# Rotary embedding on one core: the cast of the first f32 rows ahead of the position fetches on ScalarE, and a wait among GpSimd's loads

## The chip, the cores and the metric

One core of a Trainium2 chip. The metric is the device time of one execution in microseconds. Profiled times below count from the start of the span, which is 1.8 us shorter than the device time (83.6 against 85.36 us for the profiled run of before).

## The reference

```python
def reference(x, freqs, positions):          # x: 8 x 8 x 1024 x 64 f32
    half = x.shape[-1] // 2
    angles = np.outer(positions, freqs)      # 1024 x 32
    cos, sin = np.cos(angles), np.sin(angles)
    x_first, x_second = x[..., :half], x[..., half:]
    return np.concatenate([x_first * cos - x_second * sin,
                           x_first * sin + x_second * cos], axis=-1)
```

16.8 MB are read and 16.8 MB written. The sines and cosines are the same for all 64 heads, so they are computed once.

## The kernel before

The data is cut in eight tiles of 128 partitions x 64 rows x 64 values. GpSimd's loads turn f32 into bf16 on the way and its stores turn bf16 back into f32. The first 16 rows of tile 0 come by two f32 loads from SyncE and are cast by ScalarE; the last 24 rows of tile 7 (the "tail") are computed in f32 and stored by SyncE.

```python
    x0 = singles.tile([P, head, d], f32)                 # head = 16 rows, piece = 8
    for r in range(0, head, piece):
        nc.sync.dma_start(out=x0[:, r:r + piece], in_=hbm(x, 0, r, r + piece))
    # ... pos_i, fr cleared ...
    nc.scalar.dma_start(out=pos_i[...], in_=positions)   # cut
    nc.scalar.dma_start(out=fr[0:P:32], in_=freqs[None, :].to_broadcast([P // 32, half]))
    for g in range(ntiles):                              # 8 loads, one queue
        lo = 0 if g else head
        nc.gpsimd.dma_start(out=xts[g][:, lo:], in_=hbm(x, g, lo))
    # ... VectorE: shuffle pos_i and fr, turns = pos * freq / 2pi, minus its whole part ...
    nc.scalar.activation(out=sin_h, in_=turns, func=Sin, scale=twopi)
    nc.scalar.activation(out=whole, in_=turns, func=Abs)
    nc.scalar.activation(out=cos_h, in_=whole, func=Sin, scale=-twopi, bias=half_pi)
    nc.scalar.copy(out=xts[0][:, :head], in_=x0)
    # ... rotate(): four products, a difference and a sum on VectorE, per tile ...
    tail = 3 * piece
    for g in [1, 0] + list(range(2, ntiles)):
        # ... rotate, then
        nc.gpsimd.dma_start(out=hbm(out, g, 0, hi), in_=ot)
    # ... SyncE waits for the GpSimd stores but the last, then stores the tail in pieces of 8 rows
```

## Time and profile before

| | before |
|---|---|
| device time, median | 85.37 us (85.36 to 85.39, 3 runs) |
| f32 rows landed, both halves | 11.46 us |
| first product on VectorE | 17.13 us |
| loads done, last completion | 43.2 us |
| VectorE done | 73.7 us |
| DMA packets done | 82.3 us |

The prediction below shows the lines that carry the argument. The page's row of what the DMA moved in each of 40 slices (GB/s, one slice 2.09 us):

```profile
GB/s 0 182 202 259 227 208 227 204 227 208 212 220 208 227 208 227 204 212 223 200 388 423 423 455 400 470 388 463 408 439 439 416 455 423 455 392 422 431 331 70
```

Loads count on their bf16 side, so some 215 is full speed there and some 430 for stores; the step at the 21st value is where loads end and stores begin.

A line of the waits (us, times, longest): VectorE waited only 1.9 us for the frequencies, once.

```profile
DVE fr L77 <- DMA fr<-in_freqs_dram: 1.9, 1, 1.9
```

### The profile page before, as it was taken

How to read it: one execution, taken by the hardware profiler on the slowest of the kernel's cores; microseconds unless marked ns; L12 is line 12 of the kernel's file. 1: busy time of each engine (PE TensorE's matmuls, PEld its weight loads, DVE VectorE, ACT ScalarE, POOL GpSimd, SP SyncE). 2: the span in 40 equal slices, each digit the busy share in tenths (PEclk: the TensorE clock that was granted, in tenths of full speed). 3: DMA queues.
4: the chain of work that ended last, by engine and by line, in shares of the span. 5: the costliest groups of instructions: out<-in, count | busy, mean ns of one | idle time of the engine just before them, and what ended most of it. 6: DMA issues, size and time to landing. Idle time of an engine off the chain costs nothing.

```text
span 83.6 us, 163 instructions
## 1 busy us (share of the span) xinstructions
DVE 63.5 (76%) x66; ACT 9.3 (11%) x6; POOL 8.7 (10%) x20
## 2 busy tenths in 40 slices
DVE  1024995089999999999999999999999999920000
ACT  0000049999000000000000000000000000000000
POOL 4960000000002001002002002000100202000000
DMA  0899999999999999999999999999999999999992
GB/s 0 182 202 259 227 208 227 204 227 208 212 220 208 227 208 227 204 212 223 200 388 423 423 455 400 470 388 463 408 439 439 416 455 423 455 392 422 431 331 70
DMA packets 3065, 25.45 MB, mean 304 GB/s; under 512 B 360, under 2 KB 376, under 8 KB 1144
## 3 DMA queue, kind: packets, MB, share of 16 engines
q0 software_dynamic: 2304, 24.12, 94.2%
q1 hardware_dynamic: 720, 1.31, 5.1%
q10 hardware_dynamic: 40, 0.01, 0.0%
q14 instruction: 1, 0.01, 0.0%
HBM read 16.79 MB, written 16.78 MB: 402 GB/s over the span
## 4 chain that ended last, share of the span: by engine, by line
DVE 67%; DMA 12%; ACT 7%; DVEq 1%; SPq 1%; issue 0%; ACTq 0%
DMA x<-in_x_dram 12%; DVE t L114 11%; DVE t L115 11%; DVE ot L119 10%; DVE ot L117 10%; DVE ot L116 10%; DVE ot L118 10%; ACT sin_h L96 2%; ACT L96 2%; ACT L101 2%; ACT xt L101 1%; DVEq L170 1%; DVE last L117 1%; DVE last L118 1%; DVE last L116 1%; SPq L56 1%
## 5 line engine op out<-in xcount | busy, mean ns | idle before, releaser
L114 DVE TENSOR_TENSOR t<-xt,sin_h 128x2048 bf16<-128x2048 bf16 (+2 forms) x9 | 9.9, 1099 | 3.5 <-ACT sin_h L96 3.5
L128 POOL DMA_DIRECT2D out_dram<-ot x8 | 4.2, 526 | 60.4 <-DVE ot L119 60.4
L115 DVE TENSOR_TENSOR t<-xt,sin_h 128x2048 bf16<-128x2048 bf16 (+2 forms) x9 | 9.9, 1099 | 0.0
L117 DVE TENSOR_TENSOR ot<-xt,cos_h 128x2048 bf16<-128x2048 bf16 (+1 forms) x8 | 9.3, 1167 | 0.0
L119 DVE TENSOR_TENSOR ot<-ot,t 128x2048 bf16<-128x2048 bf16 (+1 forms) x8 | 9.3, 1167 | 0.0
L116 DVE TENSOR_TENSOR ot<-xt,cos_h 128x2048 bf16<-128x2048 bf16 (+1 forms) x8 | 9.3, 1166 | 0.0
L118 DVE TENSOR_TENSOR ot<-ot,t 128x2048 bf16<-128x2048 bf16 (+1 forms) x8 | 9.3, 1166 | 0.0
L74 POOL DMA_DIRECT2D xt<-in_x_dram x8 | 4.3, 577 | 0.8 <-PEq L170 0.8
L76 DVE LOAD_MASK_SELECT pos_i<-pos_i x1 | 0.0, 14 | 3.8 <-DMA pos_i<-in_positions_dram 3.8
L101 ACT ACT_TABLE_LOAD x1 | 1.3, 1283 | 11.5 <-DMA x<-in_x_dram 11.5
L87 DVE TENSOR_TENSOR turns<-pos_f,fturn 128x2048 f32<-128x2048 f32 x1 | 2.3, 2293 | 0.0
L93 DVE TENSOR_TENSOR turns<-turns,whole 128x2048 f32<-128x2048 f32 x1 | 2.3, 2293 | 0.0
L99 ACT ACTIVATE cos_h<-whole,half_pi 128x2048 bf16<-128x2048 f32 x1 | 2.0, 2003 | 0.0
L96 ACT ACTIVATE sin_h<-turns 128x2048 bf16<-128x2048 f32 x1 | 1.9, 1909 | 0.0
L98 ACT ACTIVATE whole<-turns 128x2048 f32<-128x2048 f32 x1 | 1.9, 1893 | 0.0
L77 DVE LOAD_MASK_SELECT fr<-fr x1 | 0.0, 14 | 1.9 <-DMA fr<-in_freqs_dram 1.9
L96 ACT ACT_TABLE_LOAD x1 | 1.3, 1283 | 0.0
L91 DVE TENSOR_SCALAR whole<-turns 128x2048 f32<-128x2048 f32 x1 | 1.2, 1226 | 0.0
L101 ACT CAST xt<-x 128x1024 bf16<-128x1024 f32 x1 | 1.0, 1045 | 0.0
L117 DVE TENSOR_TENSOR last<-xt,cos_h 128x768 f32<-128x768 bf16 x1 | 0.9, 950 | 0.0
L119 DVE TENSOR_TENSOR last<-last,t 128x768 f32<-128x768 f32 x1 | 0.9, 950 | 0.0
L116 DVE TENSOR_TENSOR last<-xt,cos_h 128x768 f32<-128x768 bf16 x1 | 0.9, 949 | 0.0
(12 smaller groups left out, 2.6 us busy)
## 6 DMA issues: line engine op xcount, KB each, us to landing
out_dram<-ot POOLq DMA_DIRECT2D x7, 2048.0 KB, 18.5
xt<-in_x_dram POOLq DMA_DIRECT2D x7, 1024.0 KB, 25.2
out_dram<-ot POOLq DMA_DIRECT2D x1, 1280.0 KB, 11.2
xt<-in_x_dram POOLq DMA_DIRECT2D x1, 768.0 KB, 7.6
out_dram<-last SPq DMA_DIRECT2D x3, 256.0 KB, 3.6
x<-in_x_dram SPq DMA_DIRECT2D x2, 256.0 KB, 6.9
pos_i<-in_positions_dram ACTq DMA_DIRECT2D x1, 8.0 KB, 3.7
fr<-in_freqs_dram ACTq DMA_DIRECT2D x1, 0.5 KB
```

The costliest lines, as they stand in the source:

```text
L74: nc.gpsimd.dma_start(out=xts[g][:, lo:], in_=hbm(x, g, lo))
L87: nc.vector.tensor_mul(out=turns, in0=pos_f.to_broadcast([P, C, half]), in1=fturn.to_broadcast([P, C, half]))
L93: nc.vector.tensor_sub(out=turns, in0=turns, in1=whole)
L96: nc.scalar.activation(out=sin_h, in_=turns, func=Sin, scale=twopi)
L101: nc.scalar.copy(out=xts[0][:, :head], in_=x0)
L114: v.tensor_mul(out=t1, in0=xf, in1=sin)
L115: v.tensor_mul(out=t2, in0=xs, in1=sin)
L116: v.tensor_mul(out=of, in0=xf, in1=cos)
L117: v.tensor_mul(out=os_, in0=xs, in1=cos)
L118: v.tensor_sub(out=of, in0=of, in1=t2)
L119: v.tensor_add(out=os_, in0=os_, in1=t1)
L128: nc.gpsimd.dma_start(out=hbm(out, g, 0, hi), in_=ot)
```

## The change

In short, ScalarE first casts the f32 rows and only then fetches positions and frequencies, and GpSimd queues two loads, waits for those rows, and queues the other six. The diff has a third part: the tail shrinks from 24 rows to 16.

```diff
--- before.py
+++ after.py
@@ -56,22 +56,27 @@
         nc.sync.dma_start(out=x0[:, r:r + piece], in_=hbm(x, 0, r, r + piece))
 
 
+    for g in range(ntiles):
+        lo = 0 if g else head
+        if g == 2:
+            tc.keep_in_program_order(nc.gpsimd.keepalive_nop(ins=[nc.gpsimd.lower_ap(x0)]))
+        tc.keep_in_program_order(nc.gpsimd.dma_start(out=xts[g][:, lo:], in_=hbm(x, g, lo)))
+
+
+
+    tc.keep_in_program_order(nc.scalar.copy(out=xts[0][:, :head], in_=x0))
     i32 = mybir.dt.int32
     words = mybir.dt.size(positions.dtype) // 4
     pos_i = singles.tile([P, C, words], i32)
     nc.vector.memset(pos_i, 0)
-    nc.scalar.dma_start(
+    tc.keep_in_program_order(nc.scalar.dma_start(
         out=pos_i[0:P:group].bitcast(positions.dtype),
         in_=bass.AP(tensor=positions.tensor, offset=positions.offset,
-                    ap=[[C, chunks], [1, C], [1, 1]]))
+                    ap=[[C, chunks], [1, C], [1, 1]])))
     fr = singles.tile([P, half], f32)
     nc.vector.memset(fr, 0.0)
-    nc.scalar.dma_start(out=fr[0:P:32], in_=freqs[None, :].to_broadcast([P // 32, half]))
-
-
-    for g in range(ntiles):
-        lo = 0 if g else head
-        nc.gpsimd.dma_start(out=xts[g][:, lo:], in_=hbm(x, g, lo))
+    tc.keep_in_program_order(
+        nc.scalar.dma_start(out=fr[0:P:32], in_=freqs[None, :].to_broadcast([P // 32, half])))
 
     nc.vector.stream_shuffle(pos_i, pos_i, [i // group * group for i in range(32)])
     nc.vector.stream_shuffle(fr, fr, [0] * 32)
@@ -98,8 +103,6 @@
     nc.scalar.activation(out=whole, in_=turns, func=mybir.ActivationFunctionType.Abs)
     nc.scalar.activation(out=cos_h, in_=whole, func=Sin, scale=-twopi, bias=half_pi)
 
-    nc.scalar.copy(out=xts[0][:, :head], in_=x0)
-
     v = nc.vector
 
     def rotate(g, lo, hi, ot):
@@ -118,7 +121,7 @@
         v.tensor_sub(out=of, in0=of, in1=t2)
         v.tensor_add(out=os_, in0=os_, in1=t1)
 
-    tail = 3 * piece
+    tail = 2 * piece
     ots = []
     for g in [1, 0] + list(range(2, ntiles)):
         hi = C if g < ntiles - 1 else C - tail
```

## The prediction

> **What bounds the kernel now.** I read the page's second part first, because the time before (85.37 us, with a span of 83.6 us) leaves the question whether VectorE, busy 76%, or the DMA is the bound. The rows of 40 slices (2.09 us each) answer it:
>
> ```profile
> DVE  1024995089999999999999999999999999920000
> ACT  0000049999000000000000000000000000000000
> DMA  0899999999999999999999999999999999999992
> ```
>
> The DMA is full from the second slice to the last but one; VectorE stands still in the last four slices and has holes in the first eight. The windows view (columns: busy us of each engine, clock, DMA share, GB/s) splits the DMA time:
>
> ```profile
> 2.00:42.00 40.00, 31.61 (x31) 9.32 (x6) 5.14 (x10) 1.00 1.02 215
> 42.00:82.00 40.00, 31.73 (x33) 0.00 (x0) 2.61 (x5) 1.00 1.05 421
> ```
>
> The first 40 us move the input (215 GB/s is counted on the bf16 side of the casting loads, so about 430 of f32), the second 40 us the output. Loads and big stores share one GpSimd queue, so they run in issue order. The packet records in the trace agree: loads to 42.9 us, the first store's packets from 42.4 us, and each full tile 4.86 us, load or store. So the bound is one chain of 80 us of transfers, and the printed chain that ended last (67% VectorE) is only the other long path. How far apart the two are is in the timeline:
>
> ```profile
> 17.13 1.22 DVE L114 TENSOR_TENSOR t<-xt,sin_h 128x2048 bf16<-128x2048 bf16 x1 [3.46 <-ACT sin_h L96]
> ...
> 26.59 0.54 POOL L128 DMA_DIRECT2D out_dram<-ot  x1 [21.05 <-DVE ot L119]
> ...
> 65.20 0.52 POOL L128 DMA_DIRECT2D out_dram<-ot  x1 [6.29 <-DVE ot L119]
> ...
> 69.61 0.52 POOL L128 DMA_DIRECT2D out_dram<-ot  x1 [3.89 <-DVE ot L119]
> ...
> 72.78 0.95 DVE L119 TENSOR_TENSOR last<-last,t 128x768 f32<-128x768 f32 x1
> 77.84 2.27 SPq L141 DMA_DIRECT2D out_dram<-last  x3
> ```
>
> The first store is queued at 26.59 us but moves at 42.4. This lead shrinks, because VectorE makes a tile every 6.81 us and the DMA stores one in 4.86. The seventh store, queued at 65.20, moves at 71.64; the eighth, queued at 69.61, at 76.50 (both from the packet records). VectorE could thus start late by a few microseconds at no cost. This slack decides the case.
>
> **What the Trainium skill says.**
> 1. "DMA: Bandwidth & Descriptors", Queues, rings and completion order: each DMA engine takes turns between its rows, a packet at a time. The trace agrees: the second half of the f32 rows, issued at 1.47 us, lands only at 11.46 us (the chain has "DMA x<-in_x_dram" for 9.99 us), since each of its 2 KB packets (0.09 us) takes turns with a load packet of 0.47 to 0.6 us.
> 2. "Perfetto Trace Analysis", Per-engine timelines: a ScalarE instruction is pushed into a wait queue and the sequencer goes on; a sequencer-only instruction waits on the sequencer itself. A DMA after the cast therefore need not wait for the cast to end, but does wait for a semaphore wait that stands as its own instruction. The trace has this for the f32 rows (a step "ACTq L101" of 0.02 us at 11.48, ahead of the table load). Whether a DMA passes a running activation, no line of the before trace shows.
> 3. "ScalarE: Activation LUTs", What ACT_TABLE_LOAD costs: 1283 ns, plus about 1380 ns of drain. The trace has 1283 ns twice, and no drain: the cast starts 1.30 us after its load, the sine 1.29 us after its own.
> 4. "DMA: Bandwidth & Descriptors", Where 436 GB/s comes from: a ceiling of 435 GB/s. The trace's 430 and 421 are near it, so no reordering can make the 80 us much shorter.
>
> **The change part by part.** The lines that carry it:
>
> ```profile
> 1.03 0.60 ACTq L63 DMA_DIRECT2D pos_i<-in_positions_dram  x1
> 1.27 4.27 POOL L74 DMA_DIRECT2D xt<-in_x_dram  x8 [0.83 <-PEq L170]
> 1.67 1.14 ACTq L69 DMA_DIRECT2D fr<-in_freqs_dram  x1
> 7.35 0.01 DVE L77 LOAD_MASK_SELECT fr<-fr  x1 [1.91 <-DMA fr<-in_freqs_dram]
> 11.37 2.29 DVE L93 TENSOR_TENSOR turns<-turns,whole 128x2048 f32<-128x2048 f32 x1
> 11.53 1.28 ACT L101 ACT_TABLE_LOAD   x1 [11.53 <-DMA x<-in_x_dram]
> 12.83 1.04 ACT L101 CAST xt<-x 128x1024 bf16<-128x1024 f32 x1
> 13.89 1.28 ACT L96 ACT_TABLE_LOAD   x1
> ```
>
> 1. *When the f32 rows land (X).* Before, the second half's packets began only at 5.2 us, between those of positions (3.48) and frequencies (6.16), though it was issued at 1.47. The order suggests that SyncE's and ScalarE's requests are served in turn. Without ScalarE's two, the second half should follow the first, which ends at 4.0 us: eight packets per engine, each beside a load packet, 8 x (0.47 + 0.10) = 4.6 us, to 8.6; the before run took 0.95 us from last data to landing, hence X = 9.4 us (11.5 if this reading is wrong).
>
> 2. *GpSimd's wait.* It resumes at X. Load 3 is wanted when load 2 ends, 13.1 to 13.7 us. The first load needed 2.2 us from issue to packets (1.27 to 3.50), so load 3 is ready at 11.7. Free. At X = 11.5 it would be 13.8, a hole of at most 0.6 us.
>
> 3. *Positions and frequencies.* ScalarE passes its wait at X, pushes table load and cast, and issues positions at X + 0.15, frequencies 0.65 us later. From issue to packets the idle path took 1.45 us (f32 rows: 0.75 to 2.20) and, on the full DMA, 1.6 us (last stores: 77.84 to 79.44). Then data waits for a load packet (0.3 to 0.6), the completion for another (0.6), and 0.35 us more to land: X + 3.8. Sharing a ring with positions can add up to 1 us; I take X + 4.3, so frequencies land at F = 13.7 us instead of 7.3.
>
> 4. *The angle chain.* From 7.35 to 13.66 VectorE took 6.31 us for its angle work; then the sine's 1.91 us and 0.1 of hand-overs. The sine's table load, which held the sine until 15.18 before, is over by X + 3.8 = 13.2 and leaves the path. First product at F + 8.35 = 22.05 us, late by D = 22.05 - 17.13 = 4.9 us.
>
> 5. *Tail of 16 rows instead of 24.* Start spacings give 0.069 us + 0.521 ns per bf16 element (2048: 1.136; 768: 0.469) and twice the slope for f32 output (768: 0.869). The last tile takes 6x0.736 + 2x0.469 + 4x0.869 = 8.83 us before and 6x0.869 + 2x0.336 + 4x0.602 = 8.29 after: 0.54 saved on VectorE. The eighth store grows to 48 rows and is queued 6x0.133 = 0.8 us later, at 70.41 + D. One of three last stores falls away.
>
> 6. *The end.* With 2.0 to 2.2 us from queue to packets (as the first load), store 7 can move at 67.3 + D, against 71.64: free while D is under 4.3. Store 8 can move at 72.5 + D, against 76.50: free while D is under 4.0. VectorE ends at 73.73 - 0.54 + D = 78.1, and its two last stores run beside store 8. After store 8 starts there remain 8 packets of 12 KB per engine at about 0.485 us and 16 of 2 KB at 0.086: 5.3 us, against 5.84 before (76.50 to 82.34), of which some 0.3 us are really saved. With D = 4.9: 77.4 + 5.3 + 0.2 of skew = 82.9, against 82.34: +0.6 us.
>
> Sum: nothing removed from the 80 us of transfers, about -0.3 for the smaller tail, +0.9 for the part of the delay beyond its slack. 85.37 + 0.6 = **86.0 us**.
>
> **The rivals.**
> - *ScalarE's DMA waits for the cast to finish.* The table load and cast take 1.28 + 1.05 + 0.02 us, so all moves 2.35 us: D = 7.2, time 88.2 us (+3.3%). For it: one instruction stream, and the change's own words "casts, then fetches". Against it: item 2 of the skill, with cast's inputs ready at that point.
> - *The f32 rows land no earlier (X = 11.5).* D = 7.0 and perhaps a hole in the loads: 87.9 to 88.3 us. For it: taking turns with load packets explains most of its 10 us. Against: the silent gap from 4.0 to 5.2 us. Both rivals together give some 90 us, where VectorE plainly sets the end.
> - *The fetches pass the wait.* If the separate wait is for the first half of the rows (landing at 4.55) and the cast carries the other, positions go out at 4.7, F is 9, D about 0.3, and only the tail counts: 85.0 us. Against it: before, the cast's separate wait ended at 11.46, with the second half.
> - *A gain at the start* (f32 rows unhindered, DMA full earlier): the DMA row is already 8 in its second slice, so at most about 1 us can be gained there.
>
> **Range and chances.** My reading has about half the weight, and lies between 85.2 and 86.8 with the uncertainty of F; a limit of 2% is 87.08 us. The two slower rivals have about a third, nearly all of it beyond 2%. The fetches passing the wait has a tenth. A gain of 2% would be 1.7 us of 85.4, with the transfers untouched: hardly possible. Range 85.0 to 88.3; chances 0.02 faster, 0.60 within 2%, 0.38 slower.
>
> **What would show it.** In the after timeline: table load of the cast near 9.4 us (step 1); third GpSimd load queued there and no dip in the DMA row near 13 us (2); positions issued beside the table load, not after the cast (3); frequencies' shuffle near 13.7 (3); first product near 22 us (4); last tile's pieces 128x1536 and 128x512 (5); DMA row still full or with one thin slice near 77 us, VectorE ending near 78 (6). A cast at 12.8 as before, or positions issued after the cast, makes it slower; DMA dips through the last 20 us would show VectorE as the bound.

## More of the kernel before

Next, the windows view of two stretches that turn out to matter (stretch, length, busy VectorE, ScalarE and GpSimd, clock, DMA share, GB/s):

```profile
12.00:16.00 4.00, 1.66 (x1) 3.96 (x4) 0.00 (x0) 1.00 1.04 217
40.00:46.00 6.00, 6.00 (x6) 0.00 (x0) 0.52 (x1) 1.00 1.04 343
```

In the first, two loads are done and the third begins; the second holds the turn from loads to stores.

## The result, and the profile after

The changed kernel took 88.93 us (median of 4 runs, 88.63 to 89.09), the kernel before in the same rounds 85.38 us. The ratio is 1.040, with a 95% interval of 1.036 to 1.044. It is slower by 3.6 us, outside the predicted range of 85.0 to 88.3.

The same rows of the page of the changed kernel (a slice is now 2.18 us):

```profile
DVE  0000000299919999999999999999999999999500
ACT  0000087000099500000000000000000000000000
DMA  0999999999999999999999999999999996698992
GB/s 0 217 203 244 233 205 172 200 218 203 218 207 230 203 222 222 207 215 211 154 403 414 444 437 429 437 407 452 407 456 429 399 399 264 279 452 331 435 367 72
```

Two things are new in the DMA row: thin slices at 6, 6 and 8 near its end, where VectorE is now busy almost to the end. That is a DMA that waits for VectorE. And there is a smaller dent of 172 GB/s in the seventh slice. The windows (columns as above) put numbers on it:

```profile
12.00:16.00 4.00, 0.51 (x3) 2.73 (x3) 2.70 (x6) 1.00 0.98 178
40.00:46.00 6.00, 6.00 (x6) 0.00 (x0) 0.25 (x1) 1.00 1.02 262
42.00:86.00 44.00, 39.77 (x40) 0.00 (x0) 3.14 (x6) 1.00 0.99 386
```

The output half of the run takes 44 us at 386 GB/s instead of 40 at 421. The timeline (start, length, engine, line, what, and in brackets the idle time before it and what ended it) shows what VectorE waited for:

```profile
11.12 1.28 ACT L67 ACT_TABLE_LOAD   x1 [11.12 <-DMA x<-in_x_dram]
11.19 0.60 ACTq L72 DMA_DIRECT2D pos_i<-in_positions_dram  x1
11.60 3.10 POOL L63 DMA_DIRECT2D xt<-in_x_dram  x6 [9.16 <-DMA x<-in_x_dram]
11.83 1.10 ACTq L79 DMA_DIRECT2D fr<-in_freqs_dram  x1
12.41 1.04 ACT L67 CAST xt<-x 128x1024 bf16<-128x1024 f32 x1
...
17.41 0.01 DVE L82 LOAD_MASK_SELECT fr<-fr  x1 [1.47 <-DMA fr<-in_freqs_dram]
...
25.70 1.23 DVE L117 TENSOR_TENSOR t<-xt,sin_h 128x2048 bf16<-128x2048 bf16 x1 [1.98 <-ACT sin_h L101]
...
73.78 0.52 POOL L131 DMA_DIRECT2D out_dram<-ot  x1 [6.29 <-DVE ot L122]
...
78.99 0.52 POOL L131 DMA_DIRECT2D out_dram<-ot  x1 [4.69 <-DVE ot L122]
...
81.80 1.24 SPq L144 DMA_DIRECT2D out_dram<-last  x2
```

Everything that hangs on the f32 rows starts at 11.1 us, not at 9.4 as predicted. The fetches are issued beside the table load and ahead of the cast, so they do not wait for it. The frequencies are there 5.6 us after their issue. The first product is 8.57 us late (25.70 against 17.13), and so is the store of every whole tile: the seventh is queued at 73.78 us, and by the packet records it moves at 74.87. A full store takes 4.86 us and the sixth began at 68.08, so the DMA engines that were ahead could have begun the seventh at 72.9 (the last packet of the sixth ended at 74.66): they wait for VectorE.

### The profile page after: what moved, and what is told of

It is laid out like the page before. It is cut to its first block, busy times and chain, and to the rows that moved or that the text cites. A ratio compares the mean times of both kernels' runs of the same rounds, so it can differ in the third digit from the quotient of the medians.

```text
span 87.0 us, 162 instructions
## 1 busy us (share of the span) xinstructions
DVE 63.0 (72%) x66; ACT 9.3 (11%) x6; POOL 8.7 (10%) x20
## 4 chain that ended last, share of the span: by engine, by line
DVE 71%; DMA 17%; ACT 3%; SPq 1%; DVEq 1%; issue 0%; ACTq 0%
DMA x<-in_x_dram 11%; DVE t L117 11%; DVE t L118 11%; DVE ot L120 10%; DVE ot L122 10%; DVE ot L119 10%; DVE ot L121 10%; DMA fr<-in_freqs_dram 6%; DVE turns L98 3%; DVE turns L92 3%; ACT sin_h L101 2%; DVE whole L96 1%; ACT L67 1%; SPq L56 1%; DVEq L173 1%; DVE last L120 1%
## 5 line engine op out<-in xcount | busy, mean ns | idle before, releaser
L67 ACT ACT_TABLE_LOAD x1 | 1.3, 1283 | 11.1 <-DMA x<-in_x_dram 11.1
L101 ACT ACT_TABLE_LOAD x1 | 1.3, 1283 | 0.0
L120 DVE TENSOR_TENSOR last<-xt,cos_h 128x512 f32<-128x512 bf16 x1 | 0.7, 689 | 0.0
L122 DVE TENSOR_TENSOR last<-last,t 128x512 f32<-128x512 f32 x1 | 0.7, 689 | 0.0
```

The costliest lines, as they stand in the source:

```text
L67: tc.keep_in_program_order(nc.scalar.copy(out=xts[0][:, :head], in_=x0))
L120: v.tensor_mul(out=os_, in0=xs, in1=cos)
L122: v.tensor_add(out=os_, in0=os_, in1=t1)
```

## The experiments

Twelve kernels ran, all correct; six of them are the remaining combinations of the change's three parts. Kernels ran together with new runs of the kernel before, whose medians were 85.28 to 85.41 us. "First product" is the start of VectorE's first product in the profiled run, "loads done" the last completion of the eighth load in the trace.

| kernel | tail | fetches | GpSimd's wait | first product | loads done | time, median |
|---|---|---|---|---|---|---|
| before | 24 | first | none | 17.13 | 43.24 | 85.38 |
| tail alone | 16 | first | none | 17.12 | 43.24 | 85.39 |
| wait alone | 24 | first | third load | 17.11 | 45.86 | 87.73 |
| wait and tail | 16 | first | third load | 16.59 | 46.48 | 88.01 |
| late fetches alone | 24 | after rows | none | 26.06 | 43.43 | 89.99 |
| late fetches and tail | 16 | after rows | none | 26.04 | 43.54 | 89.17 |
| late fetches and wait | 24 | after rows | third load | 26.04 | 45.89 | 89.63 |
| changed | 16 | after rows | third load | 25.70 | 45.88 | 88.93 |

### Fetches first again (wait and tail kept)

```diff
-    tc.keep_in_program_order(nc.scalar.copy(out=xts[0][:, :head], in_=x0))
     ... the two fetches on ScalarE ...
+    tc.keep_in_program_order(nc.scalar.copy(out=xts[0][:, :head], in_=x0))
```

> The changed kernel with the cast moved behind the two fetches on ScalarE, so positions and frequencies are fetched at once again; GpSimd's wait and the tail of 16 rows stay. Theory (the late fetches alone cost the 3.6 us, by starting the products 8.6 us late): frequencies land near 7.3 us, first product near 17 us, time 85.0 to 85.6 us. Rival (GpSimd's wait, which leaves a hole in the loads near 13 us and lets one DMA engine trail, costs a part): 86 to 88 us although the first product is at 17 us.

Measured: 88.01 us (87.63 to 88.30, 4 runs), ratio to before 1.031 (1.028 to 1.034). The first product is back at 16.59 us and VectorE ends at 72.7, yet the time falls by only 0.9 us. That is at the upper edge of the rival's range. My theory, that the late fetches alone cost the 3.6 us, fell here in its simple form: with them undone, something else holds the end.

### The wait alone

```diff
     for g in range(ntiles):
         lo = 0 if g else head
+        if g == 2:
+            tc.keep_in_program_order(nc.gpsimd.keepalive_nop(ins=[nc.gpsimd.lower_ap(x0)]))
-        nc.gpsimd.dma_start(...)
+        tc.keep_in_program_order(nc.gpsimd.dma_start(...))
```

> The kernel before with GpSimd's wait ahead of the third load alone. Theory: hole of 0.2 to 0.7 us in the loads, which the full DMA cannot give back: 85.4 to 86.1 us. Rival (the wait costs a good part of the 3.6 us): 86.5 us or more. VectorE's first product stays at 17.1 us either way.

Measured: 87.73 us (87.11 to 88.42), ratio 1.028 (1.022 to 1.033). The rival held. Its windows:

```profile
12.00:16.00 4.00, 1.83 (x1) 3.96 (x4) 3.10 (x6) 1.00 1.00 188
40.00:46.00 6.00, 6.00 (x6) 0.00 (x0) 0.52 (x1) 1.00 0.98 238
```

From 12 to 16 us the DMA moves 188 GB/s instead of 217: 0.5 us of work lost on average (4 us x 29/217). But a load is done only when the last of its 16 parts is. The Trainium skill ("DMA: Bandwidth & Descriptors", Why a DMA increments its semaphore by 16 and not by 1) says that each of the 16 DMA engines posts its own completion, and the trace has 16 completion records for every load. Before, those of the third load lie between 18.30 and 18.84 us; with the wait, between 18.67 and 19.86, so the last is 1.0 us late. The gap stays through the seventh load (39.33 against 38.30): nothing evens the engines out here. At the turn from loads to stores another 1.6 us are lost (last completion of the eighth load 45.86 against 43.24, 238 GB/s instead of 343), with single packets of up to 1.6 us where 0.63 is usual. This second loss is not only the latest part's: the earliest part of the eighth load is 1.6 us late too (44.42 against 42.82). The stores then follow at the old pace, and the whole end is 2.4 us later.

### The wait one load later

```diff
-        if g == 2:
+        if g == 3:
```

> The kernel before with GpSimd's wait for the f32 rows ahead of the fourth load, so three loads are queued instead of two. Theory (the wait costs because two loads run out at 13 us, just as the third is being queued, and a DMA engine that falls behind there stays behind): the queue never runs dry, the loads end near 42.9 us as before, time 85.2 to 85.7 us. Rival (the stop and restart of GpSimd's issuing costs by itself, or waiting on the rows does): about 87 to 88 us as with the wait ahead of the third load.

This is the kernel with the wait alone, but with three loads queued ahead of it. Measured: 85.33 us, ratio 1.000 (0.998 to 1.002). Its windows are close to those of before:

```profile
12.00:16.00 4.00, 1.49 (x1) 3.96 (x4) 1.88 (x4) 1.00 1.08 225
40.00:46.00 6.00, 6.00 (x7) 0.00 (x0) 0.52 (x1) 1.00 1.06 337
```

So neither the wait nor the restart of GpSimd's issuing costs; letting the queue run dry does. Two loads last until 12.8 to 13.7 us, and the third was issued at 12.0 us with the wait alone, with its first packet at 13.2 (11.6 and 12.8 in the changed kernel).

### The late fetches alone

```diff
-        if g == 2:
-            tc.keep_in_program_order(nc.gpsimd.keepalive_nop(...))       # in the changed kernel
-    tail = 2 * piece
+    tail = 3 * piece
```

> The changed kernel without GpSimd's wait and with the tail of 24 rows of before, so only the order on ScalarE is changed. Theory: first product 8 to 9 us late as in the changed kernel, and VectorE's end, now 0.5 us later for the larger tail, sets the time: 89.0 to 89.7 us. Rival (the wait carries a part): 86 to 88 us.

Measured: 89.99 us (89.86 to 90.07), ratio 1.054 (1.052 to 1.056). Without any wait, and with the loads done at 43.43 us as before, it is slower than the changed kernel, and slightly more than expected. Two lines of its timeline matter for the fetches:

```profile
11.06 0.60 ACTq L70 DMA_DIRECT2D pos_i<-in_positions_dram  x1
16.77 0.01 DVE L79 LOAD_MASK_SELECT pos_i<-pos_i  x1 [15.72 <-DMA pos_i<-in_positions_dram]
```

The positions are the first request on ScalarE's queue, and yet they take 5.7 us. Their first packet moves at 14.92 us, 3.86 us after the issue. In the changed kernel, where GpSimd's third load is issued only after them (11.60 against 11.19 us), it is 1.59 us.

### The changed kernel with the old tail

```diff
-    tail = 2 * piece
+    tail = 3 * piece
```

> The changed kernel with the tail of 24 rows of before. If VectorE sets the end of the changed kernel, its 0.54 us more of work show fully or are partly given back by the smaller eighth store: 89.0 to 89.6 us. If the DMA still sets the end, it is the 0.3 us of a third small store: 89.2 us at most, with no later VectorE end visible in the time. The same as the changed kernel (88.9) would say that the tail is worth nothing in this state.

Measured: 89.63 us (89.59 to 89.85), ratio 1.051. The smaller tail goes with 0.7 us by the medians and 1.06 by the profiled runs (89.85 - 88.79), of which 0.34 is a later first product in this run (26.04 against 25.70). What is left, 0.4 to 0.7 us, is about VectorE's 0.5: VectorE sets the end here.

### The changed kernel without its wait

```diff
-        if g == 2:
-            tc.keep_in_program_order(nc.gpsimd.keepalive_nop(ins=[nc.gpsimd.lower_ap(x0)]))
```

> The changed kernel with GpSimd's wait taken out and nothing else, which completes the table of four at a tail of 16 rows: neither part 85.39, wait alone 88.01, both 88.93. If the later of two ends counts (the wait's cost lies under the late fetches'), taking the wait out gives nothing back: 88.7 to 89.3 us. If the two costs add, it gives back some 2.5 us: about 86.4 us.

Measured: 89.17 us (89.09 to 89.48), ratio 1.045. Taking the wait out of the changed kernel gives nothing back. Together with the table this shows how the two costs go together: alone they cost 2.6 us (wait and tail, 88.01 - 85.39) and 3.8 us (late fetches and tail, 89.17 - 85.39), together 3.5 us. They do not add; the later end counts. The end of this kernel:

```profile
74.11 0.52 POOL L129 DMA_DIRECT2D out_dram<-ot  x1 [6.29 <-DVE ot L120]
79.33 0.52 POOL L129 DMA_DIRECT2D out_dram<-ot  x1 [4.69 <-DVE ot L120]
...
82.14 1.24 SPq L142 DMA_DIRECT2D out_dram<-last  x2
```

Each of the last stores is issued as soon as VectorE has its data, 0.33 us later than in the changed kernel, as the first product is.

### All loads behind the wait

```diff
-        if g == 2:
+        if g == 0:
```

> The changed kernel with GpSimd's wait ahead of its first load, so the f32 rows have the DMA to themselves (wrong as a design, right as a measurement). Theory A: the second half's packets still start near 5.3 us, rows land near 6.5. Theory B: they start right behind the first half's at about 3.9 us, rows land near 5.5. Time about 90 us, as the DMA stands idle for some 5 us, though the fetches come early.

The changed kernel with the DMA left to the f32 rows. Time 89.09 us (state unknown, one run), about 90 expected. What it is for is the second half of the rows. The view by tile of the f32 rows gives issue to landing (minimum, median, maximum):

```profile
DMA to landing us min/median/max: 3.6/3.7/3.8
```

The second half lands 3.8 us after its issue instead of 9.6 (changed kernel) or 10.0 (before), and by the packet records its packets start at 3.46 us, right behind the first half's, instead of at 5.4. So theory B: the 1.4 us gap is made by GpSimd's load packets, and ScalarE's fetches have no part in it.

### The second half from ScalarE's queue

```diff
-    for r in range(0, head, piece):
-        nc.sync.dma_start(out=x0[:, r:r + piece], in_=hbm(x, 0, r, r + piece))
+    nc.sync.dma_start(out=x0[:, :piece], in_=hbm(x, 0, 0, piece))
+    tc.keep_in_program_order(
+        nc.scalar.dma_start(out=x0[:, piece:], in_=hbm(x, 0, piece, head)))
```

> The changed kernel with the second 8 f32 rows fetched from ScalarE's queue at the start. Theory A (a load behind another of the same queue starts only about when the first has landed, 4.5 us plus some 0.8): as the first of its queue its packets start near 3.5 us and the rows land near 9 us, time about 87. Theory B (the load packets of GpSimd that start at 3.2 us are taken in a first batch ahead of it): packets start at 5.3 us as before, landing at 11 us, time about 88.9.

Measured: 85.86 us (one look, state unknown), and the rows landed at 6.0 us. Packets started at 3.27 us, as theory A had it, but the landing is far earlier than either theory said: it moved ahead of GpSimd's loads, whose packets now began only at 4.69 us. Neither theory is right as I wrote it. The edit changed two things at once: the half is first on its queue, and it is issued at 0.74 us instead of 1.47, so before GpSimd's first load (1.27). The positions decide what matters: first on ScalarE's queue but behind queued loads, their first packet came 3.83 to 4.08 us after the issue (rows in one, late fetches alone, changed kernel without its wait); issued ahead of the load that GpSimd held back, it came after 1.38 to 1.59 us (all loads behind the wait, changed kernel with either tail) or 2.67 us (frequencies from SyncE's queue). So a request that is issued behind queued loads starts late even when it is first on its queue.

### The rows in one load

```diff
-    for r in range(0, head, piece):
-        nc.sync.dma_start(out=x0[:, r:r + piece], in_=hbm(x, 0, r, r + piece))
+    nc.sync.dma_start(out=x0, in_=hbm(x, 0, 0, head))
```

> The changed kernel with the 16 f32 rows fetched by one load instead of two of 8 rows. In all traces the second half's packets start only near 5.3 us although it is issued at 1.47. If that gap belongs to the second request, one load has no gap: the rows land at 5 to 8 us instead of 11.05, GpSimd goes on before the queue is dry, frequencies land 3 to 6 us earlier, and the time falls to 85 to 87 us. If it is only the taking of turns with the load packets (16 turns of 0.57 us whatever their size would be 8 here): 8 to 9 us and 86 to 87.5 us. The same 11 us and 88.9 us if neither counts.

Measured: 85.44 us (85.35 to 85.64), ratio 1.0005 (0.999 to 1.002). This one line takes the whole loss of the changed kernel away. The view by tile of the f32 rows:

```profile
DMA to landing us min/median/max: 5.2/5.2/5.2
```

They land at 5.9 us instead of 11.05: the whole request is issued at 0.74 us, before GpSimd's first load (1.27). GpSimd issues its third load at 6.5, long before the queue is dry. The frequencies land soon enough for a first product at 20.65 us, still 3.5 us later than before, and that costs nothing: the slack that the prediction claimed is there.

### Frequencies from SyncE's queue

```diff
-        nc.scalar.dma_start(out=fr[0:P:32], in_=freqs[None, :].to_broadcast([P // 32, half])))
+    tc.keep_in_program_order(nc.sync.keepalive_nop(ins=[nc.sync.lower_ap(x0)]))
+        nc.sync.dma_start(out=fr[0:P:32], in_=freqs[None, :].to_broadcast([P // 32, half])))
```

> The changed kernel with the frequencies fetched from SyncE's queue, behind the same wait for the f32 rows, so at the same time as the positions and not second on ScalarE's queue. In the changed kernel they were issued at 11.83 us and landed at 17.4, 6.3 us after the rows, where the prediction had 4.3. If being second in the queue is what costs, they land near 15 us, the first product comes near 23.5 us, 2 us earlier, and the time falls to about 87 us. If it is the frequencies' own request that is slow (its issue takes 1.1 us against 0.6), they land at 16.5 to 17 us, and the time is 88.0 to 88.7 us.

Measured: 87.39 us (median of the three fast runs, 87.34 to 87.90; a fourth was slow), ratio of fast runs 1.026 (1.022 to 1.029). Timeline:

```profile
11.42 0.61 SPq L80 DMA_DIRECT2D fr<-in_freqs_dram  x1
11.48 0.56 ACTq L72 DMA_DIRECT2D pos_i<-in_positions_dram  x1
...
13.97 0.01 DVE L83 LOAD_MASK_SELECT fr<-fr  x1 [12.92 <-DMA fr<-in_freqs_dram]
...
15.74 0.01 DVE L82 LOAD_MASK_SELECT pos_i<-pos_i  x1 [1.34 <-DMA pos_i<-in_positions_dram]
```

The frequencies are there 2.55 us after their issue instead of 5.6. It is not their own request that is slow. But the edit changed two things again: they are first on their queue, and they are issued at 11.42 us, ahead of GpSimd's third load (11.89) and not behind it (11.83 against 11.60). So it is not shown that being second was what cost. In the kernels where both fetches stand behind queued loads, the frequencies, second on the queue, needed only 0.7 to 1.1 us more from issue to first packet than the positions, first on it (4.56 to 4.97 against 3.83 to 4.08). The positions (4.3 us) are now the last to come, and the first product starts at 24.16 us, 1.5 us earlier than in the changed kernel. The time fell by 1.5 us as well, so VectorE still sets the end, with the end that the wait alone gives (87.73) close under it: the loads of this kernel ran dry too and were done at 45.66 us.

### The smaller tail alone

```diff
-    tail = 3 * piece
+    tail = 2 * piece
```

> The kernel before with the tail of 16 rows alone: one small store fewer where the DMA sets the end. By the prediction's step 6 it saves up to 0.3 us: 85.0 to 85.3 us. If the tail is worth something only where VectorE sets the end: 85.4 us.

Measured on the kernel before: 85.39 us (85.28 to 85.59, 6 runs), ratio 1.0005 (0.9985 to 1.0025). Where the DMA sets the end, the smaller tail is worth nothing; the 0.3 us that the prediction gave it are not there.

### A try at beating both: no small stores

```diff
-    tail = 3 * piece
-        hi = C if g < ntiles - 1 else C - tail
+    # all 64 rows of every tile by rotate() and GpSimd's store; no f32 tail, no SyncE stores
```

> A try at beating both: the kernel before with all 64 rows of the last tile stored by GpSimd from bf16, no f32 tail and no small stores. The last 2.1 MB took 5.84 us before (76.50 to 82.34) and a full tile takes 4.86, so up to 1 us less of transfers; VectorE has 8 us to spare. Expected 84.5 to 85.0 us; about 85.4 if the big store's completion comes as much later as the transfers end earlier.

Measured: 85.75 us (85.66 to 85.86, 6 runs), ratio 1.004 (1.002 to 1.006): a miss, slightly slower. The packets of the last store end at 82.25 us, 0.1 earlier than before, but the span then lasts another 1.83 us (84.08 - 82.25) instead of 1.24 (83.58 - 82.34). No kernel beats the one before; those that keep the DMA full (85.3 to 85.4) all end with it.

## Why the prediction was wrong

Its mechanism for the size of the loss was right: the loss is the delay of VectorE's first product beyond a slack that it has against the DMA. It chose 86.0 us because it put that delay at 4.9 us; it was 8.57.

1. *When the f32 rows land: the step failed.* Predicted 9.4 us, with 11.5 as a rival, measured 11.05. The step laid the late start of the second half to ScalarE's two requests. They were gone in the changed kernel and its packets still started at 5.37 us. The looks without loads beside it (landing at 5.3) and with the half on ScalarE's own queue (6.0) show that it is GpSimd's load packets: the second half is issued at 1.47 us, behind the first load (1.27), and its packets start 3.9 us later, against 2.0 us without loads beside it. This is 1.65 us of the 3.7 missing.

2. *GpSimd's wait: called free, or at most a 0.6 us hole. It failed as a step, and it did not decide the result.* The mean hole was 0.5 us, as the rival said. But alone it cost 2.4 us. Up to 1.0 us of this is the latest of 16 parts, which stays behind; the rest is lost at the turn to the stores, for a reason that stays open. In the changed kernel this lies under VectorE's later end: taking the wait out changed 88.93 to 89.17. The seventh store's wait for VectorE also lets the engines draw level there (the parts of the sixth store land 1.65 us apart, those of the seventh 0.34).

3. *The fetches: half right.* They did not wait for the cast, as step 3 and the second point of the prediction's list from the Trainium skill had it ("Perfetto Trace Analysis", Per-engine timelines): issued at 11.19 us, 0.07 after the table load's start. That settles what no line of before showed. But the frequencies landed 6.3 us after the rows, not 4.3. The step that failed is the time from issue to first packet: it had 1.6 us on the full DMA, and up to 1 us more for sharing with the positions. The positions kept to it (1.59 us); the frequencies, issued at 11.83 us behind GpSimd's third load (11.60), needed 4.53. As far as the runs separate the two causes, loads queued ahead cost 1.2 to 2.7 us (3.83 to 4.08 for the positions against 1.38 to 2.67) and second place 0.7 to 1.1. This is the other 2.0 us.

4. *The angle chain: right.* From landing to first product 8.31 us (17.39 to 25.70), predicted 8.35.

5. *The tail: right on VectorE, wrong on the DMA.* Some 0.5 us where VectorE sets the end, nothing where the DMA does.

6. *The end: the slack was mis-sized the other way.* From queueing to packets the step took 2.0 to 2.2 us from the very first load; on the seventh store it is 1.09 (73.78 to 74.87). (The Trainium skill, "DMA: Bandwidth & Descriptors", Specifications, has about 1 us to the first byte on this path; the seventh store agrees, the first load does not.) The eighth store thus has 76.50 - 70.41 - 1.09 = 5.0 us of slack instead of 4.0. Check: late by 8.57 less 5.0 is 3.6 us; measured 3.5 over the kernel with the tail alone. Late by 8.9 (the changed kernel without its wait) less 5.0 is 3.9; measured 3.8. Late by 3.5 (rows in one): predicted none, measured none. Late by 7.0 (frequencies from SyncE's queue) less 5.0 is 2.0; measured 2.0.

   The check holds for the tail of 16 rows only. With 24 rows the eighth store has 76.50 - 69.61 - 1.09 = 5.8 us of slack, and late by 8.93 (late fetches alone) would give 88.5 us; measured 89.99. There the small stores, issued at 82.68 us when VectorE was done, moved at 83.93, after the last packet of the eighth store (83.53): their path sets the end, and the prediction's sum does not have it.

With the measured delay put in, the prediction's own sum would have said some 4.2 us of loss, or 3.2 with the shorter latency. The choice among rivals was the fault: the second rival (rows at 11.5, 87.9 to 88.3 us) was the nearest, and it too lacked the slow second fetch.

One reading of the prediction is weaker than it looks. The 435 GB/s of its item 4 are, in the section that it cites, the ceiling of the ports of SBUF, the on-chip memory. There the tiles are bf16, and the loads move 215 GB/s; its 430 and 421 are counted in f32. That the transfers fill the 80 us is shown by the full DMA row, not by this comparison.

What stays open: why the turn from loads to stores loses another 1.1 to 1.6 us in every kernel whose queue ran dry, and not in the rows-in-one kernel, whose parts are 1.1 to 1.2 us apart too; whether it is one DMA engine that stays behind, since the records do not name it; and how much of the delay of the f32 rows and of the frequencies is second place on the queue, since each run that took the place away also moved the request ahead of a GpSimd load.

## What to carry to other kernels

Here a queue that ran dry for half a microsecond on average cost 2.4 us at the end; keep one transfer more queued than the wait seems to need. A small fetch is slow when it is issued behind queued full-rate loads (3.8 to 4.1 us to its first packet here, against 1.4 to 2.7 ahead of them), rather than for its size; issue fetches that feed a long chain ahead of the loads, and first on their queue. And before undoing one of two suspected causes, ask which sets the end: here each part alone costs most of the loss, and undoing only one gives 0.9 us or nothing back.

## What the Trainium skill lacked or had wrong

- "DMA: Bandwidth & Descriptors", Issuing engines are not separate DMA queues, says that issuing from several engines saves only sequencer time, usually little. Here that time was worth more: issued from ScalarE at 0.74 us instead of 1.47 from SyncE, the second half of the f32 rows came ahead of GpSimd's first load (1.27) and landed at 6.0 us instead of 11.05.
- The same page, Queues, rings and completion order: turns between rows explain the pace of the second half (packets of 0.09 us from 5.4 to 10.0 us), but not its start 3.9 us after issue beside loads, against 2.0 us (1.47 to 3.46) without them. The positions show the same: 3.83 to 4.08 us behind queued loads, 1.38 to 2.67 ahead of them.
- No page says that a short starvation of the queue sets the parts of a transfer apart and that they stay apart: third load 18.67 to 19.86 us with the wait alone, 18.30 to 18.84 before; seventh load 38.42 to 39.33 against 37.75 to 38.30.
- "ScalarE: Activation LUTs", What ACT_TABLE_LOAD costs, adds about 1380 ns of drain to the 1283 ns of every switch to a different set. In the changed kernel the cast starts 1.29 us after its table load (11.12 to 12.41), and in the kernel before the sine 1.29 us after its own (13.89 to 15.18): no such drain shows.
- "Perfetto Trace Analysis", Per-engine timelines, does not say outright whether a DMA issued from ScalarE passes a queued activation; here it was issued 1.22 us ahead of the cast that stands before it in the program.
